# Two Strassen groups of 512 + 512 columns, the last of B's queries among them; heads of both branches in turn with fewer products between; branch A's rotary embedding on GpSimd

## The chip, the cores and the metric

The kernel runs on one core of one Trainium2 chip. The metric is the device time of one execution in microseconds (us); the median of three runs counts.

## The reference, cut to what matters

One encoder block with two token mixers in parallel: branch A is differential attention (8 heads, each with two 64-wide halves), branch B is grouped-query attention (8 query heads over 2 key/value heads) with normed q and k and a two-dimensional rotary embedding. All projections come from one matrix of 2048 x 10752.

```python
h = rmsnorm(x, norm_g)                                   # x: 512 x 2048, float32
qa, ka, va, za, qb, kb, vb, zb, ga, gb = split(h @ w_in) # w_in: 2048 x 10752
qa, ka = apply_rope(qa, ang_1d), apply_rope(ka, ang_1d)
oa = rmsnorm(diff_attention(qa1, qa2, ka1, ka2, va, lam), subln_g) * (1 - lam_init)
ya = (oa * silu(za)) @ w_out_a                           # 1024 x 2048
qb, kb = axial_rope(rmsnorm(qb)), axial_rope(rmsnorm(kb))
yb = (gqa_attention(qb, kb, vb) * silu(zb)) @ w_out_b    # 1024 x 2048
x = x + (sigmoid(ga) * ya + sigmoid(gb) * yb) @ w_o      # 2048 x 2048
return rmsnorm(x, final_g)
```

`apply_rope` is `x * cos` plus the other half of `x` times a signed `sin`: two multiplications and one addition per element.

## The kernel before

Every float32 factor of a large product is split into a high part (`hi`, rounded to the matmul type fp32r, a cast on ScalarE, L103) and a low part (`lo`, what is left, a subtraction on VectorE, L104). One product then takes three matmuls: high by high, low by high, high by low. A weight piece of 512 KB (tile `w_raw`, 128 x 1024) is loaded by an SP queue, cast to `w_hi` and subtracted to `w_lo`; eight `w_raw` buffers (named in the list `slots`) are used in turn.

The program has five stages. First (0 to 69 us of the span) x is loaded, normed and transposed, and four column blocks of 128 are projected. Second, up to 714.5 us, comes the Strassen stage (`strassen`, matmul line L234): each group takes 256 + 256 columns of `w_in` as 2 x 2 quarters and forms 7 products instead of 8. There are four groups of columns (`STRASSEN_BLOCKS`: V of branch A, K and V of B, and B's query blocks 28 to 31), and twelve groups for the gates z and g. A product is 48 matmuls with a moving side of 256 columns for the column groups (x is the stationary side), and 48 as well for the gates, 336 in a group. The `b` quarters are loaded once; differences of quarters (`sub`, L209) are made on VectorE in the place of the loaded ones.

Third is attention (714.5 to 1119 us). The order of TensorE's work is written out by hand here (`manual_schedule`); the other engines' order is set by the scheduler of the language. The sixteen heads come in the order `HEADS`. For each head, TensorE does the scores of four row blocks, the transposes that turn a later head's q (`turn`), the transposes of this head's probabilities (`turn_p`, L608), and later, after the next head's first two score blocks, the product with V (`attend`, L621). Between these pieces stand steps of other work, taken from `fillers()` by `fill(n)`: the three digits of a head in `FILLS` are the steps after `finish` of the head before, before `turn_p`, and after `turn_p`. A step is 12 matmuls of 512 columns or 24 of 256. The middle digit is what TensorE has to do while the last row block of scores is reduced (max), exponentiated and scaled on VectorE and ScalarE, since the fourth transpose of `turn_p` needs that row block.

The steps come from `FILL_BLOCKS`: eight pairs of column blocks of `w_in` with 8 steps each (branch A's q and k blocks as pairs of rows, 96 matmuls of 512 columns; B's query blocks 32, 33 and 34, 35 as pairs of columns, 192 matmuls of 256 columns), and then 32 steps of the output projection `w_out_b`. For `w_out_b`, B's head results (`og`) have to be split into hi and lo first; they fall in the last pair's steps.

`load_roped` prepares q and k of a head of branch A: it loads a block, loads it a second time with its halves exchanged, and does the rotary embedding in place with three `tensor_tensor` of 128 x 512 on VectorE (L546 to L548). It is called twice per head, two heads ahead. Branch B's rotary embedding (`rope_b`) is on VectorE too; the reciprocal root of its norm is two small operations on GpSimd (`rsqrt_pool`, L99 and L100). The last multiplication of an A head (L700) is on GpSimd.

Fourth is `w_out_a` (1119 to 1199 us), fifth the output projection `w_o` in four Strassen groups with the final norm.

The PSUM tiles `acc` and `aux` are eight banks, shared out anew by `share_banks` in each stage.

Of the kernel before, what the change touches and what calls it, by code (L numbers as in the profile page):

```python
# [45 lines left out]
FILLS = "141 141 131 131 030 021 032 142 121 350 121 131 332 331 222 232".split()  # L46
# [3 lines left out]
def hybrid_block_kernel(  # L50
# [8 lines left out]
    nc = tc.nc  # L59
# [4 lines left out]
    ps_pool = ctx.enter_context(tc.tile_pool(name="ps", bufs=1, space=bass.MemoryType.PSUM))  # L64
    banks = {}

    def share_banks(**kw):
        banks.update(kw)

    def bank(kind, shape):  # L70
        ring = banks[kind]
        ring.append(ring.pop(0))
        return ps_pool.tile([P, *shape], F32, name=kind, tag=f"bank{ring[-1]}")

    def acc_tile(*shape):
        return bank("acc", shape)
# [201 lines left out]

    zg = dram.tile([2 * BW, S], F32, name="zg")
# [209 lines left out]

# [45 lines left out]
    def load_roped(b):  # L535
# [550 lines left out]
```

## Time and profile before

| what | us |
|---|---|
| median of 3 runs (1374.53 to 1377.92) | 1374.69 |
| the profiled execution's own time | 1376.67 |
| its span in the trace | 1374.9 |
| Strassen stage | 69.4 to 714.5 |
| attention stage | 714.5 to 1119.0 |
| `w_out_a`, then `w_o` | 1119.0 to 1374.9 |

The span is the time from the first to the last instruction. PE is TensorE, DVE VectorE, ACT ScalarE, POOL GpSimd and SP SyncE, which issues the transfers. In a row of instructions the form is: line, engine, operation, output<-inputs, shape, count. Where a view gives `a, b, c` after a wait, those are the total, the number and the longest.

### The profile page before, as it was taken

Reading aid. Unit: us, or ns where it says so; the run is one execution under the profiler, and the core shown is the slowest. Engines: PE = TensorE matmul, PEld = TensorE weight load, DVE = VectorE, ACT = ScalarE, POOL = GpSimd, SP = SyncE. Lnnn points to the kernel's source line nnn. Section 1 sums busy time; section 2 is a strip of 40 time slices with the busy share of each in tenths; the row PEclk is TensorE's granted clock in tenths of the full one; section 3 lists DMA queues with packets and bytes.
Section 4 is the critical chain, followed back from the end, with each engine's and each line's share of the span. In section 5 each row is a group of like instructions: output and inputs, shape, how many; then the busy total and the mean of one; then the engine's idle time right before and its main releaser. Section 6 shows DMA issues by size and latency. Waiting matters only on the chain.

```text
span 1374.9 us, 24100 instructions
## 1 busy us (share of the span) xinstructions
PE 1350.2 (98%) x9625; PEld 1274.1 (93%) x9625; DVE 1081.1 (79%) x1400; ACT 702.9 (51%) x1110; POOL 84.5 (6%) x94
## 2 busy tenths in 40 slices
PE   6999999999999999999999999999999999999997
PEld 6999999999999999999998888888788888899997
DVE  5977787777777777777759778787898858899886
ACT  7643333444444444444446675575676753354444
POOL 1000000000000000000003201000000010004322
PEclk9999999999999999999999999999999999999999
DMA  8245434543333444333377454545575446463333
GB/s 291 77 147 161 124 116 149 154 146 113 118 121 123 148 149 143 117 122 118 123 207 220 122 154 147 153 139 162 171 221 182 130 145 202 151 245 116 97 95 123
DMA packets 201743, 204.21 MB, mean 149 GB/s; under 512 B 11280, under 2 KB 175392, under 8 KB 200992
## 3 DMA queue, kind: packets, MB, share of 16 engines
q1 hardware_dynamic: 201632, 202.69, 47.5%
q8 instruction: 75, 1.23, 0.4%
q14 instruction: 36, 0.29, 0.1%
HBM read 165.68 MB, written 32.77 MB: 144 GB/s over the span
## 4 chain that ended last, share of the span: by engine, by line
PE 90%; DVE 4%; ACT 2%; DMA 1%; issue 1%; POOL 0%; SPq 0%; DVEq 0%; POOLq 0%; ACTq 0%
PE acc L234 55%; PE acc L175 27%; PE aux L621 3%; PE aux L608 2%; PE aux L739 1%; DVE w_lo L104 1%; PE aux L664 1%; PE aux L665 1%; DVE w_raw L209 1%; DMA rows<-og 1%; DMA xt<-in_x_dram 1%; PE aux L389 0%; DMA rows<-yg 0%; ACT sq L366 0%; ACT w_hi L103 0%
## 5 line engine op out<-in xcount | busy, mean ns | idle before, releaser
L103 ACT CAST w_hi<-w_raw 128x1024 fp32r<-128x1024 f32 x351 | 368.5, 1050 | 516.8 <-PE acc L234 397.9
L104 DVE TENSOR_TENSOR w_lo<-w_raw,w_hi 128x1024 fp32r<-128x1024 f32 x351 | 431.9, 1232 | 168.7 <-ACT w_hi L103 168.2
L209 DVE TENSOR_TENSOR w_raw<-w_raw 128x1024 f32<-128x1024 f32 x160 | 200.0, 1250 | 2.4
L234 PE MATMUL acc<-a2h,w_hi 128*128 128x256 f32 x384 | 108.7, 283 | 0.0
L234 PE MATMUL acc<-a2l,w_hi 128*128 128x256 f32 x384 | 108.7, 283 | 0.0
L234 PE MATMUL acc<-a2h,w_lo 128*128 128x256 f32 x384 | 108.7, 283 | 0.0
L234 PEld LDWEIGHTS acc<-a2h,w_hi 128*128 128x128 f32 x384 | 73.7, 192 | 0.0
L234 PEld LDWEIGHTS acc<-a2l,w_hi 128*128 128x128 f32 x384 | 73.7, 192 | 0.0
L234 PEld LDWEIGHTS acc<-a2h,w_lo 128*128 128x128 f32 x384 | 73.7, 192 | 0.0
L576 DVE TENSOR_REDUCE nmax<-aux 128x1 f32<-128x512 f32 x96 | 61.0, 681 | 7.5 <-PE aux L739 4.7
L175 PE MATMUL acc<-a1h,w_hi 128*128 128x512 f32 (+1 forms) x160 | 56.6, 358 | 0.2 <-ACT a1h L393 0.2
L175 PE MATMUL acc<-a1l,w_hi 128*128 128x512 f32 (+1 forms) x160 | 55.6, 353 | 0.1
L175 PE MATMUL acc<-a1h,w_lo 128*128 128x512 f32 (+1 forms) x160 | 55.7, 353 | 0.0
L175 PE MATMUL acc<-a2l,w_hi 128*128 128x512 f32 (+1 forms) x160 | 55.5, 348 | 0.0
L175 PE MATMUL acc<-a2h,w_hi 128*128 128x512 f32 (+1 forms) x160 | 55.5, 350 | 0.0
L175 PE MATMUL acc<-a2h,w_lo 128*128 128x512 f32 (+1 forms) x160 | 55.4, 347 | 0.0
L234 PE MATMUL acc<-s4h,w_lo 128*128 128x256 f32 x192 | 54.3, 283 | 0.0
L234 PE MATMUL acc<-a1h,w_hi 128*128 128x256 f32 x192 | 54.3, 283 | 0.0
L234 PE MATMUL acc<-a1l,w_hi 128*128 128x256 f32 x192 | 54.3, 283 | 0.0
L234 PE MATMUL acc<-a1h,w_lo 128*128 128x256 f32 x192 | 54.3, 283 | 0.0
L234 PE MATMUL acc<-s1h,w_hi 128*128 128x256 f32 x192 | 54.3, 283 | 0.0
L234 PE MATMUL acc<-s1l,w_hi 128*128 128x256 f32 x192 | 54.3, 283 | 0.0
(325 smaller groups left out, 4356.0 us busy)
## 6 DMA issues: line engine op xcount, KB each, us to landing
w_raw<-in_w_in_dram SPq DMA_DIRECT2D x136, 512.0 KB, 3.6
w_raw<-in_w_in_dram SPq DMA_DIRECT2D x64, 256.0 KB, 3.7
w_raw<-in_w_o_dram SPq DMA_DIRECT2D x32, 512.0 KB, 4.4
gg<-kept SPq DMA_DIRECT2D x32, 256.0 KB, 2.4
w_raw<-in_w_out_b_dram SPq DMA_DIRECT2D x32, 256.0 KB, 3.5
rows<-gg SPq DMA_DIRECT2D x32, 256.0 KB, 3.4
w_raw<-in_w_out_a_dram SPq DMA_DIRECT2D x32, 256.0 KB, 3.4
cols<-pv SPq DMA_DIRECT2D x26, 256.0 KB, 3.3
```

The source lines that it names most:

```text
L103: nc.scalar.copy(out=hi, in_=src)
L104: nc.vector.tensor_tensor(out=lo, in0=src, in1=hi.bitcast(F32), op=ALU.subtract)
L175: nc.tensor.matmul(out=acc[b][:, place], lhsT=l, rhs=r, start=first and kc == order[0] and k == 0 and i == 0, stop=last and kc == order[-1 ...
L209: nc.vector.tensor_tensor(out=d, in0=u, in1=v, op=ALU.subtract)
L234: nc.tensor.matmul(out=ps[u] if by_row else ps[:, u, :], lhsT=l, rhs=r, start=n % (2 if by_row else 4) == 0 and k == 0 and i == 0, stop=n ...
L576: nc.vector.tensor_reduce(out=nmax, in_=sps, axis=AX.X, op=ALU.max, negate=True)
L608: nc.tensor.transpose(out=tp[:, i * P:(i + 1) * P], in_=self.p[i][:, j * P:(j + 1) * P], identity=ident)
L621: nc.tensor.matmul(out=o, lhsT=l, rhs=r, start=j == 0 and i == 0, stop=j == NT - 1 and i == 2)
L664: nc.tensor.matmul(out=sp, lhsT=qs[:, sl], rhs=kh, start=True, stop=False)
L665: nc.tensor.matmul(out=sp, lhsT=qs[:, sl], rhs=kl, start=False, stop=True)
L739: nc.tensor.matmul(out=sp, lhsT=l, rhs=r, start=n == 0, stop=n == 2)
```

## The change

Two of the three column groups after the first, 20 to 27 and 28 to 35 instead of 20 to 23, 24 to 27 and 28 to 31, are formed by a new function `strassen_wide` of 512 + 512 columns. A quarter is 1024 x 512 in four pieces of 512 KB; a product is 48 matmuls of 512 columns with the other factor stationary, and is held in a two-bank PSUM tile. Two of the quarter sets use `w_raw` buffers, a third a pool of its own (`wide`), and the quarter b21 is loaded again for the last product. The first of the two groups (`late`) forms p5 before p2.

B's query blocks 32 to 35 thereby leave `FILL_BLOCKS`, which has six pairs (48 steps) instead of eight (64). `HEADS` has the heads of A and B in closer turn, and `FILLS` has 65 steps after the first 8 instead of 89, so that 7 steps of `w_out_b` are left after the last head (before: none). The rotary embedding of branch A is done by GpSimd. PSUM pools are opened anew for each stage (`new_banks`).

```diff
-STRASSEN_BLOCKS = [(16, 17, 18, 19), (20, 21, 22, 23), (24, 25, 26, 27), (28, 29, 30, 31)]
-FILL_BLOCKS = [(32, 33), (2, 10), (3, 11), (34, 35), (4, 12), (5, 13), (6, 14), (7, 15)]
-HEADS = "B0 B1 A0 B2 B3 B4 B5 A1 A2 B6 B7 A3 A4 A5 A6 A7".split()
+STRASSEN_BLOCKS = [(16, 17, 18, 19)]
+
+WIDE_BLOCKS = [tuple(range(20, 28)), tuple(range(28, 36))]
+FILL_BLOCKS = [(2, 10), (3, 11), (4, 12), (5, 13), (6, 14), (7, 15)]
+HEADS = "B0 B1 A0 B2 B3 A1 B4 B5 A2 B6 A3 B7 A4 A5 A6 A7".split()
...
-FILLS = "141 141 131 131 030 021 032 142 121 350 121 131 332 331 222 232".split()
+FILLS = "121 111 121 111 111 121 111 111 121 111 121 111 222 222 222 222".split()
...
+    def strassen_wide(w, left, right, act, wide, done, late=False):
+        H = NK // 2
+        def load(q, half, pieces):
+            tiles = []
+            for p in range(4):
+                if q < 2:
+                    r = raw_tile(q * 4 + p, (2, S))
+                else:
+                    r = wide.tile([P, 2, S], F32, name="w_raw", tag=f"w_wide{p}")
...
+        def product(name, b):
+            ps = acc_tile(2, S)
+            ah, al = act[name]
+            for p in range(4):
+                hi, lo = split_w(b[p])
+                for u in range(2):
+                    sl = slice(u * P, (u + 1) * P)
+                    for k in range(2):
+                        kk = p * 2 + k
+                        for i, (l, r) in enumerate(((ah, hi), (al, hi), (ah, lo))):
+                            nc.tensor.matmul(out=ps[:, u, :], lhsT=l[:, kk, sl], rhs=r[:, k, :],
+                                             start=kk == 0 and i == 0, stop=kk == H - 1 and i == 2)
+            return ps
...
+        b11, b12 = load(0, 0, left), None
+        if late:
+            b12 = load(1, 0, right)
+        b21 = load(2, 1, left)
+        b12 = b12 or load(1, 0, right)
+        p1 = product("a11", b11)
+        u = tmp("u")
+        nc.scalar.copy(out=u, in_=p1)
+        if not late:
+            p2 = product("a12", b21)
+            b22 = load(2, 1, right)
+        sub(b11, b12, b11)
+        p5 = product("s1", b11)
+        if late:
+            p2 = product("a12", b21)
+            b22 = load(2, 1, right)
+        done(0, 0, plus(tmp("c"), p2, u))
+        sub(b11, b22, b11)
+        p6 = product("s2", b11)
+        plus(u, p6, u)
+        t = plus(tmp("t"), p5, u)
+        sub(b12, b22, b12)
+        p3 = product("s3", b12)
+        b21 = load(1, 1, left)
+        plus(u, p3, u)
+        done(1, 1, plus(tmp("c"), p5, u))
...
+        done(0, 1, plus(t, product("s4", b22), t))
+        sub(b21, b21, b11)
+        done(1, 0, plus(u, product("a22", b21), u))
...
+        with tc.tile_pool(name="wide", bufs=1) as wide:
+            for n, blocks in enumerate(WIDE_BLOCKS):
+                def kept(th, ch, v, blocks=blocks):
+                    keep_cols(blocks[ch * 4:ch * 4 + 4], th * 2, 2, v)
+                strassen_wide(w_in, column_pieces(blocks[:4]), column_pieces(blocks[4:]), xq, wide, kept, late=n == 0)
...
-        nc.vector.tensor_tensor(out=o, in0=o, in1=sa, op=ALU.mult)
-        nc.vector.tensor_tensor(out=v, in0=v, in1=ca, op=ALU.mult)
-        nc.vector.tensor_tensor(out=v, in0=v, in1=o, op=ALU.add)
+        nc.gpsimd.tensor_tensor(out=o, in0=o, in1=sa, op=ALU.mult)
+        nc.gpsimd.tensor_tensor(out=v, in0=v, in1=ca, op=ALU.mult)
+        nc.gpsimd.tensor_tensor(out=v, in0=v, in1=o, op=ALU.add)
```

TensorE's list of instructions has 9152 rows before and 8432 after. In the column groups VectorE's order changes most. Before, a 256 + 256 group reads like this on VectorE (`w_lo` are splits, `w_raw<-w_raw` differences of quarters, `kept<-acc,kept` the sums of products):

```order
L104 TENSOR_TENSOR w_lo<-w_raw,w_hi 128x1024 x2
L209 TENSOR_TENSOR w_raw<-w_raw 128x1024 x2
L104 TENSOR_TENSOR w_lo<-w_raw,w_hi 128x1024
L432 TENSOR_TENSOR kept<-acc,kept 128x512
L209 TENSOR_TENSOR w_raw<-w_raw 128x1024
L104 TENSOR_TENSOR w_lo<-w_raw,w_hi 128x1024
L209 TENSOR_TENSOR w_raw<-w_raw 128x1024
L104 TENSOR_TENSOR w_lo<-w_raw,w_hi 128x1024 x3
L240 TENSOR_TENSOR kept<-acc,kept 128x512 x2
L104 TENSOR_TENSOR w_lo<-w_raw,w_hi 128x1024 x2
L240 TENSOR_TENSOR kept<-acc,kept 128x512
L432 TENSOR_TENSOR kept<-acc,kept 128x512
```

After, the first wide group from the splits of its second product's quarter on (`wide_c` and `wide_u` are the sums, 128 x 1024 now):

```order
L112 TENSOR_TENSOR w_lo<-w_raw,w_hi 128x1024 x6
L310 TENSOR_TENSOR w_raw<-w_raw 128x1024
L112 TENSOR_TENSOR w_lo<-w_raw,w_hi 128x1024
L310 TENSOR_TENSOR w_raw<-w_raw 128x1024 x2
L112 TENSOR_TENSOR w_lo<-w_raw,w_hi 128x1024
L310 TENSOR_TENSOR w_raw<-w_raw 128x1024 x2
L112 TENSOR_TENSOR w_lo<-w_raw,w_hi 128x1024 x2
L310 TENSOR_TENSOR w_raw<-w_raw 128x1024
L330 TENSOR_TENSOR wide_c<-acc,wide_u 128x1024
L112 TENSOR_TENSOR w_lo<-w_raw,w_hi 128x1024
L310 TENSOR_TENSOR w_raw<-w_raw 128x1024
L112 TENSOR_TENSOR w_lo<-w_raw,w_hi 128x1024
```

Differences of quarters now alternate with splits piece by piece, since a quarter has four pieces, and the two L240/L432 sums of 128 x 512 are one L330 sum of 128 x 1024.

The second place is VectorE from the second pair of row blocks of head B5 to the four `pl` that follow its `turn_p` (`nmax` is the row maximum, `rs` one over the sum, `kl` the low part of A's keys, `pl` that of the turned probabilities). Before:

```order
L576 TENSOR_REDUCE nmax<-aux 128x1 x2
L578 TENSOR_TENSOR nmax<-nmax,ssb 128x1
L104 TENSOR_TENSOR kl<-kd,kh 128x512
L578 TENSOR_TENSOR nmax<-nmax,ssb 128x1
L546 TENSOR_TENSOR other<-other,sa 128x512
L744 RECIPROCAL rs<-ssum 128x1 x2
L104 TENSOR_TENSOR w_lo<-w_raw,w_hi 128x1024
L547 TENSOR_TENSOR cols<-cols,ca 128x512
L104 TENSOR_TENSOR pl<-aux,ph 128x512 x4
L548 TENSOR_TENSOR cols<-cols,other 128x512
```

After:

```order
L681 TENSOR_REDUCE nmax<-aux 128x1 x2
L683 TENSOR_TENSOR nmax<-nmax,ssb 128x1
L112 TENSOR_TENSOR kl<-kd,kh 128x512
L683 TENSOR_TENSOR nmax<-nmax,ssb 128x1
L849 RECIPROCAL rs<-ssum 128x1 x2
L112 TENSOR_TENSOR w_lo<-w_raw,w_hi 128x1024
L112 TENSOR_TENSOR pl<-aux,ph 128x512 x4
```

The three rotary operations L546 to L548 are gone from between; the split of `kl` and that of a weight piece stand where they stood.

The third place is GpSimd in the middle of the heads, where `ssb` is the norm of a B head (L99 and L100, now L107 and L108). Before:

```order
L99 TENSOR_SCALAR ssb<-ssb 128x4
L100 TENSOR_TENSOR ssb<-ssb,neg_half 128x4
L700 TENSOR_TENSOR rows<-y_9156,rows 128x512
L99 TENSOR_SCALAR ssb<-ssb 128x4
L100 TENSOR_TENSOR ssb<-ssb,neg_half 128x4
```

After:

```order
L652 TENSOR_TENSOR cols<-cols,ca 128x512
L107 TENSOR_SCALAR ssb<-ssb 128x4
L108 TENSOR_TENSOR ssb<-ssb,neg_half 128x4
L652 TENSOR_TENSOR cols<-cols,ca 128x512
L651 TENSOR_TENSOR other<-other,sa 128x512
L653 TENSOR_TENSOR cols<-cols,other 128x512
```

The rotary operations (now L651 to L653) stand between the two small operations that the B heads' scores need.

## Rows read from the trace of the kernel before

**Rows 1.** The page, busy time of each engine, share of the span, instructions.

```profile
PE 1350.2 (98%) x9625; PEld 1274.1 (93%) x9625; DVE 1081.1 (79%) x1400; ACT 702.9 (51%) x1110; POOL 84.5 (6%) x94
```

**Rows 2.** Stretches: window, length, busy us (count) per engine, PEclk, DMA share, GB/s.

```profile
core 0: us, PE busy (x) PEld busy (x) DVE busy (x) ACT busy (x) POOL busy (x), PEclk, DMA share, GB/s
...
69.40:714.50 645.10, 645.10 (x5378) 645.10 (x5378) 485.72 (x466) 273.16 (x294) 0.00 (x0) 1.00 0.44 136
734.80:920.00 185.20, 184.71 (x999) 159.78 (x998) 146.46 (x282) 121.58 (x268) 14.89 (x15) 0.99 0.53 157
...
1000.00:1119.00 119.00, 118.83 (x563) 98.91 (x562) 105.23 (x180) 84.18 (x164) 6.03 (x4) 1.00 0.56 173
```

**Rows 3.** The chain that ended last, in order: start, us, what.

```profile
714.50 17.29 PE acc L175 x144
...
733.61 1.20 PE aux L587 x8
...
747.97 10.90 PE acc L175 x48
...
1118.96 79.37 PE acc L175 x350
```

**Rows 4.** Waits of TensorE between 714 and 1120 us.

```profile
PE aux L587 <- ACT w_hi L103: 1.8, 1, 1.8
PE acc L175 <- ACT og1h L103: 0.5, 1, 0.5
PE aux L608 <- DVE p L555: 0.5, 1, 0.5
```

**Rows 5.** Groups by form, 690 to 1130 us: busy, mean ns | idle before.

```profile
L548 DVE TENSOR_TENSOR cols<-cols,other 128x512 f32<-128x512 f32 x16 | 12.0, 752 | 0.2
L546 DVE TENSOR_TENSOR other<-other,sa 128x512 f32<-128x512 f32 x16 | 10.9, 680 | 1.8 <-DMA other<-pv 1.8
L547 DVE TENSOR_TENSOR cols<-cols,ca 128x512 f32<-128x512 f32 x16 | 10.9, 684 | 8.4 <-DMA cols<-pv 8.4
...
L700 POOL TENSOR_TENSOR rows<-y,rows 128x512 f32<-128x512 f32 x8 | 13.5, 1686 | 292.8 <-DVE y L699 175.9 <-DMA w_raw<-in_w_out_b_dram 74.3 <-DMA w_raw<-in_w_out_a_dram 29.1
```

**Rows 6.** Groups by form: 400 to 600 us (first row), 1246 to 1263 us (others).

```profile
L209 DVE TENSOR_TENSOR w_raw<-w_raw 128x1024 f32<-128x1024 f32 x40 | 48.8, 1220 | 0.7
...
L209 DVE TENSOR_TENSOR w_raw<-w_raw 128x1024 f32<-128x1024 f32 x6 | 9.4, 1574 | 0.0
L104 DVE TENSOR_TENSOR w_lo<-w_raw,w_hi 128x1024 fp32r<-128x1024 f32 x5 | 8.7, 1759 | 0.0
L944 POOL TENSOR_TENSOR xrh<-xrh,gf 128x256 f32<-128x256 f32 x6 | 8.1, 1369 | 123.0 <-DMA gf<-in_final_g_dram 120.7 <-ACT acc L923 2.3
L944 POOL TENSOR_TENSOR xrl<-xrl,gf 128x256 f32<-128x256 f32 x4 | 6.8, 1721 | 0.0
```

**Rows 7.** GpSimd and VectorE side by side (timeline: start, us, what), and GpSimd alone.

```profile
827.07 2.20 POOL L700 TENSOR_TENSOR rows<-y,rows 128x512 f32<-128x512 f32 x1 [41.38 <-DVE y L699]
...
828.05 1.77 DVE L548 TENSOR_TENSOR cols<-cols,other 128x512 f32<-128x512 f32 x1
...
933.19 1.30 POOL L700 TENSOR_TENSOR rows<-y,rows 128x512 f32<-128x512 f32 x1 [70.19 <-DVE y L699]
```

**Rows 8.** Timeline: last score matmul and last scaling, heads B4, B7 and A6.

```profile
853.50 0.39 PE L739 MATMUL aux<-kbl,qh 128*128 128x512 f32 x1
...
860.10 0.48 DVE L555 TENSOR_SCALAR p<-p,rs 128x512 f32<-128x512 f32 x1
...
970.97 0.40 PE L739 MATMUL aux<-kbl,qh 128*128 128x512 f32 x1
...
974.12 0.49 DVE L555 TENSOR_SCALAR p<-p,rs 128x512 f32<-128x512 f32 x1
...
1074.35 0.39 PE L665 MATMUL aux<-kl,qs 128*128 128x512 f32 x1
...
1080.35 0.74 DVE L673 SCALAR_TENSOR_TENSOR p<-e,rs,p 128x512 f32<-128x512 f32 x1
```

**Rows 9.** Loads of weight pieces: KB each, us to landing; and SyncE's waits, 60 to 700 us.

```profile
w_raw<-in_w_in_dram SPq DMA_DIRECT2D x136, 512.0 KB, 3.6
...
SPq L203 <- DVE w_lo L104: 213.8, 107, 2.8
```

More of the change, by code (lines that the diff above doesn't have):

```diff
@@ L62, in hybrid_block_kernel, with new_banks @@
     dram = ctx.enter_context(tc.tile_pool(name="dram", bufs=1, space=bass.MemoryType.DRAM))
-    ps_pool = ctx.enter_context(tc.tile_pool(name="ps", bufs=1, space=bass.MemoryType.PSUM))
+    ps_pools = ctx.enter_context(ExitStack())
     banks = {}
+    def new_banks(unit):
+        ps_pools.close()
+        banks["pool"] = unit, ps_pools.enter_context(
+            tc.tile_pool(name="ps_" + unit, bufs=1, space=bass.MemoryType.PSUM))
     def share_banks(**kw):
@@ L72, in bank @@
         ring.append(ring.pop(0))
-        return ps_pool.tile([P, *shape], F32, name=kind, tag=f"bank{ring[-1]}")
+        unit, pool = banks["pool"]
+        return pool.tile([P, *shape], F32, name=kind, tag=f"{unit}{ring[-1]}")
     def acc_tile(*shape):
@@ L116, in split_w @@
         if free is None:
-            hi = wp.tile(shape, F32R, name="w_hi", tag="w_hi")
-            lo = wp.tile(shape, F32R, name="w_lo", tag="w_lo")
+            hi, lo = (wp.tile(shape, F32R, name=n, tag=n) for n in ("w_hi", "w_lo"))
         else:
@@ L277, in strassen, with sub, tmp, plus @@
         slots[:] = o[1] + o[0] + o[3] + o[2]
+    def strassen_wide(w, left, right, act, wide, done, late=False):
[7 more added lines that the diff above has]
+                    r = wide.tile([P, 2, S], F32, name="w_raw", tag=f"w_wide{p}")
+                row, at = (half * H + p * 2) * P, 0
+                for c0, n in pieces:
+                    nc.sync.dma_start(out=r[:, :, at:at + n],
+                                      in_=w[row:row + 2 * P, c0:c0 + n].rearrange("(k p) n -> p k n", p=P))
+                    at += n
+                tiles.append(r)
+            return tiles
+        def sub(dst, x0, x1):
+            for d, u, v in zip(dst, x0, x1):
+                nc.vector.tensor_tensor(out=d, in0=u, in1=v, op=ALU.subtract)
+        def product(name, b):
[11 more added lines that the diff above has]
+            return ps
+        def tmp(tag):
+            return wide.tile([P, 2, S], F32, name="wide_" + tag, tag="wide_" + tag)
+        def plus(dst, ps, sb):
+            nc.vector.tensor_tensor(out=dst, in0=ps, in1=sb, op=ALU.add)
+            return dst
+        b11, b12 = load(0, 0, left), None
[24 more added lines that the diff above has]
+        done(1, 1, plus(tmp("c"), p5, u))
+        if late:
+            ring = banks["acc"]
+            ring[0], ring[1] = ring[1], ring[0]
+        done(0, 1, plus(t, product("s4", b22), t))
+        sub(b21, b21, b11)
+        done(1, 0, plus(u, product("a22", b21), u))
@@ L336, in plain_rows @@
         return stream_steps(w_in, column_pieces(blocks), NK, False, act, kept, **kw)
+    new_banks("bank")
     share_banks(acc=[0, 1, 2, 3], aux=[4, 5, 6, 7])
@@ L453, in hybrid_block_kernel @@
             project(STRASSEN_BLOCKS[0], early, in_xt, before={"s2": late_sums})
+        slots[:] = slots[2:4] + slots[0:2] + slots[4:]
+        new_banks("pair")
+        share_banks(acc=[2, 3, 0, 1])
+        with tc.tile_pool(name="wide", bufs=1) as wide:
[3 more added lines that the diff above has]
+                strassen_wide(w_in, column_pieces(blocks[:4]), column_pieces(blocks[4:]), xq, wide, kept, late=n == 0)
+        slots[:] = slots[0:2] + slots[4:6] + slots[2:4] + slots[6:8]
         with tc.tile_pool(name="sp", bufs=6) as sp:
+            new_banks("bank")
+            free = [2 * i + j for i in banks["acc"] for j in range(2)]
+            share_banks(acc=free[:4])
             def tmp():
```

## Prediction

> **What bounds the kernel now.** I read four views in this order. The page's busy times show TensorE at 98% of the span and VectorE at 79% [rows 1], so the sum starts with TensorE's work, and VectorE is what can get in its way. The stretches say where: in the Strassen stage TensorE is busy for all of the 645.10 us, with VectorE at 485.72 (75%); among the heads (734.8 to 920) TensorE has 184.71 of 185.20 and VectorE 79%; from 1000 to 1119 VectorE has 105.23 of 119.00, 88% [rows 2]. TensorE's waits in the attention stage are few: 1.8 us before B0's transposes, one 0.5 for the last scaling of a head's probabilities, one 0.5 for the splits of the head results [rows 4]. [...] The chain gives the pace of a matmul by its width.
>
> **Matmuls removed.** A matmul of 256 columns takes 645.10 / 5378 = 120.0 ns in the Strassen stage [rows 2] and 17.29 / 144 = 120.1 in the first steps of attention; one of 512 columns takes 10.90 / 48 = 227.1, or 79.37 / 350 = 226.8 over the longest piece [rows 3]; I take 226.9. So two narrow ones cost 240, one wide one 227. Of the column groups, three leave: 3 x 336 = 1008 narrow matmuls, 121.0 us. Two pairs of B's queries leave the steps: 2 x 192 = 384 narrow ones, 46.1 us. Two wide groups come: 2 x 7 x 48 = 672 wide ones, 152.5 us. Net **-14.6 us** on the engine that sets the end: 5.8 of the 46.1 is Strassen's eighth product, the rest the fixed part of each matmul. TensorE's list loses just these 720 rows, and no other matmul changes.
>
> **Cover in the heads.** 16 steps (64 - 48) and the order of the heads change what lies between a head's last score matmul and the fourth transpose of its `turn_p`. For seven of the eight B heads (all but B0) the middle digit falls to 1: 12 wide matmuls, 2.73 us, and 0.33 until the fourth transpose. To this come 0.44 where the next head is a B, whose q is turned there (4 transposes at 109 ns), and 0.45 where the head before is an A, whose norm has two matmuls there. So the cover is 3.06 for B1, B3 and B5, 3.5 for B6 and B7, 3.95 for B2 and B4, 3.44 in the mean. Against it stands the latency from the issue end of the last score matmul (its start plus 0.23) to the end of the last scaling. B7 shows the shortest of before, 974.61 - 971.20 = 3.41, and B4 the longest, 860.58 - 853.73 = 6.85 [rows 8]: between B4's two rows VectorE ran almost without a gap through work of others. In the new order nothing but one `kl` (0.68) or one weight split (1.22) stands in the way, partly beside the exponential on ScalarE, and the rotary operations that stood there have gone. Adding these per head by the order's rows gives latencies of 4.15 (B1), 4.6 (B2), 3.55 (B3), 4.15 (B5), 4.0 (B6), and 3.5 or less for B7 and under the cover for B4; less the covers that is 1.1 + 0.65 + 0.5 + 1.1 + 0.5 = 3.85 us. The 0.5 that B4 waits now goes [rows 4]. Net **+3.3**; bounds 0 (all at 3.41: 3 x 0.35, less the 0.5) and 23.9 (all at 6.85: 7 x 3.41). I take the low part since the rows that made B4 slow are those that move to GpSimd.
>
> Six A heads come newly to two middle steps, 5.46 + 0.33 + 0.45 = 6.24 us. A6 has that cover now and takes 1081.09 - 1074.58 = 6.51 [rows 8], a wait of 0.27. Six times that is **+1.6**, bounds 0 and 5. The splits of B's results for `w_out_b` (`og1h`, `og1l`) fall between B7 and A4, in fewer steps than before; they cost one wait of 0.5 [rows 4]. VectorE is the fullest engine in that region [rows 2]; I take three such waits, **+1.5**, bounds 0 and 6.
>
> **Start of the heads.** From the last gate product (714.50) to B0's transposes (733.61) pass 19.1 us for B0's loads, tables and norm [rows 3], and that does not change. The six steps ahead of them shrink from 17.29 to 72 x 0.2271 = 16.35, so TensorE waits **+0.9** longer there, at the most. At the end the seven `w_out_b` steps that the heads now leave over run at the same pace behind them: 0.
>
> **Wide groups.** VectorE has per wide group 28 splits, 16 differences and 6 sums of 128 x 1024, about 50 x 1.22 = 61 us [rows 6] in 336 x 0.2269 = 76.2 of TensorE, 80%; before it was 75% and TensorE waited nowhere [rows 2]. Loads of 512 KB need 3.6 us to land and already wait 107 times for a split to free their buffer [rows 9]. New is that b22 goes into the buffers of b21, issued only when b21 is split, and b21 comes a second time into those of b12, while VectorE, in order, holds a difference that needs them. One product (10.9 us) lies between; a margin of about 1 us is left by the order's rows, so **+1**, bounds 0 and 8 (four fills of a third buffer set, each 2 us late, by the spread of one load).
>
> **Rotary on GpSimd.** VectorE loses 12.0 + 10.9 + 10.9 = 33.8 us and two in-order waits for transfers, 8.4 and 1.8 [rows 5]. GpSimd gets 48 operations of 128 x 512: 1.30 us alone, 2.20 beside VectorE [rows 7], 1.69 in the mean [rows 5], so 62 to 106 us in 400, on an engine that is 6% busy [rows 1]; loads two heads ahead hide them. What they do to VectorE is the open price. Beside GpSimd's multiplications of `xrh` and `xrl` (14.9 us in all), VectorE's subtraction goes from 1220 ns to 1574 and its split to 1759 [rows 6]: eleven operations lose 6 x 0.354 + 5 x 0.54 = 4.8 us, for GpSimd work that alone would be ten times some 0.74, an estimate from half of the 1.30 for half the columns and a fixed part: 7.4 us, so 0.65 us lost per us. A rotary addition took 1.77 beside GpSimd instead of 0.68 [rows 7, 5]. For 62 us that is between 0, if they fall beside VectorE's reading of PSUM and its idle time, and 40. About half of VectorE's time among the heads goes to operations of two operands from SBUF, so I take 20: VectorE still gains 34 + 10 (eight weight splits fewer) - 20. For the single late scaling that falls beside one: **+1**, bounds 0 and, for all of it, the case below.
>
> [...]
>
> **Sum.** -14.6 + 3.3 + 1.6 + 1.5 + 0.9 + 1 + 1 = -5.3 us. The profiled execution's own time is 1376.67 for a span of 1374.9, 2.0 above the median; taken from the median of 1374.7, that is **1369.4 us** (from the profiled execution 1371.4).
>
> **Rivals.**
> (1) The covers hold: latencies near B7's 3.41 and VectorE relieved; 14.6 less 0.9 and some 0 to 3: 1360 to 1364. For it: the rotary rows lie in B4's slow stretch. Against: a cover of 3.06 is under the shortest latency seen.
> (2) VectorE loses the whole 40 us by GpSimd, 20 more than in the sum. Then relief and loss cancel while TensorE has 30 us less in which to hide VectorE's work; of the 20 a third to two thirds falls into the covers: +7 to +13, 1376 to 1382. For it: rows 6. Against: GpSimd's work can fall where VectorE reads PSUM.
> (3) Slower: each of the seven B heads waits in the short cover. The place is the transposes of `turn_p`, the price 7 x (latency - 3.44). The other terms leave 14.6 + 0.5 - 6.0 = 9.1 us to lose, so it decides from a mean latency of 4.75, and the time is over 1378.8 from 5.35. At 5.5, between B7's and B4's: +14.4, 1380. For it: B4's 6.85 with a short cover in the same place. Against: that stretch held the rotary operations.
> (4) The wide groups wait for their late loads at the bound, +8 instead of +1: 1376. Against: no wait on a load in 645 us [rows 2].
>
> **How the numbers follow.** A measurement of this kernel can tell 0.3% from no change: below 1370.6 is faster, above 1378.8 slower. My forecast (1364 to 1373): 0.42, of it 0.32 faster and 0.10 same. (1): 0.20, faster. (2): 0.15, 0.08 same and 0.07 slower. (3): 0.17, 0.05 same and 0.12 slower. (4): 0.06, same. Together 0.52 faster, 0.29 same, 0.19 slower. The range goes from the full gain of (1), 1360, to 1381, past most of (2) and half of (3).
>
> **What would show it.** Matmuls: the column groups take about 152 us in two pieces at 227 ns, without waits. Covers: TensorE's waits L713 <- `p` in the attention stage sum to about 5 us over the B and A heads; 12 or more is (3), under 2 is (1). GpSimd: about 70 to 90 us busy in the heads, and VectorE's `w_lo` among the heads above 1.22 us; at 1.6 or more in the mean it is (2). Wide groups: waits on `w_lo` or on loads of more than 4 us make (4). The forecast is wrong if TensorE's waits in all exceed 13 us more than now, or if the wide matmul's pace in a two-bank tile isn't 227 ns.

## The result

The changed kernel takes 1415.79 us (median of 4) against 1374.99 for the kernel before in the same series: 1.0298 times as long, 95% interval 1.0285 to 1.0311. That is 41 us slower, far outside the predicted range of 1360 to 1381. The profiled execution took 1416.43, its span is 1414.5.

The page of the changed kernel, its engine line and the row of TensorE's clock, beside [rows 1]:

```profile
PE 1350.8 (95%) x8905; PEld 1240.2 (88%) x8905; DVE 1091.4 (77%) x1359; ACT 707.3 (50%) x1111; POOL 152.0 (11%) x142
...
PEclk9999999999999999999999999999789999999999
```

720 matmuls are gone and TensorE is still as long busy (1350.8 for 1350.2), now at 95% instead of 98%: those that are left ran slower in places. The last row is the granted clock in forty slices, in tenths; two of them are at 0.7 and 0.8. The waits of TensorE from 60 us on (engine, what it waited for: total, number, longest), beside [rows 4]:

```profile
PE acc L182 <- ACT og1h L111: 19.0, 5, 10.5
PE aux L713 <- ACT p L658: 7.6, 6, 5.0
PE aux L713 <- DVE p L660: 5.6, 6, 1.5
PE aux L692 <- DMA cols<-pv: 3.6, 1, 3.6
PE aux L713 <- DVE p L778: 1.8, 2, 0.9
PE acc L241 <- DVE wide_u L330: 1.6, 1, 1.6
PE acc L322 <- DVE xt L522: 1.4, 1, 1.4
```

Five waits on `og1h`, the high part of B's head results for `w_out_b`, are the largest item; before, there was one, of 0.5. Fourteen waits before turned probabilities (L713) come next. Three stretches of the changed kernel, beside [rows 2] (the wide groups, the first half of the heads, and the place of the `og1h` waits):

```profile
110.00:264.00 154.00, 152.65 (x675) 126.15 (x673) 119.25 (x103) 60.92 (x58) 0.00 (x0) 1.00 0.53 162
764.00:960.00 196.00, 181.57 (x850) 149.88 (x849) 161.66 (x294) 133.19 (x301) 72.08 (x63) 0.96 0.50 148
1000.00:1035.00 35.00, 16.90 (x57) 11.59 (x56) 14.99 (x28) 12.52 (x26) 7.05 (x5) 0.66 0.44 130
```

The wide groups run almost without a gap. Among the heads TensorE stands 14 us of 196, and in 35 us around 1017 it is busy for 16.9, at a mean granted clock of 0.66 (PEclk is 0.50 from 1008.9 to 1032.8, 1.00 before and behind).

I added up the distances from one matmul's start to the next over the whole span, subtracted the pace of its width at full clock (the prediction's), and sorted what is left by place. Distances at half clock count apart.

| part, us | before | after | change | predicted |
|---|---|---|---|---|
| matmuls at their pace | 1287.3 | 1272.7 | -14.6 | -14.6 |
| waits in the Strassen stage | 0 | 4.5 | +4.5 | +1 |
| wait at the start of the heads | 2.0 | 3.75 | +1.75 | +0.9 |
| transposes of probabilities, B heads | 0.7 | 15.95 | +15.3 | +3.3 and +1 |
| the same, A heads | 0.3 | 2.1 | +1.8 | +1.6 |
| `og1h`, `og1l` before `w_out_b` | 1.3 | 20.6 | +19.2 | +1.5 |
| other waits among the heads | 2.4 | 4.4 | +2.0 | |
| slower matmuls at half clock | 1.5 | 10.8 | +9.3 | none |

The sum is +39.3; the spans differ by 39.6.

**The longest wait.** The chain of the changed kernel (start, us, what) from the last multiplication of head A3 on:

```profile
1006.88 1.28 POOL rows L805
...
1008.17 3.16 DMA og<-rows
...
1011.39 2.87 DMA rows<-og
...
1014.28 0.63 ACT og1h L111
...
1014.93 0.70 DVE og1l L112
...
1015.65 2.67 DMA rows<-og
...
1018.35 0.63 ACT og1h L111
```

A3's result is multiplied in its `z` buffer, stored (3.16 us), and only then does the first reload of an earlier B head's result start, in that buffer: 2.87 us to load, 0.63 and 0.70 to split. The next reload starts when that split has ended, again in the same buffer, since the other `z` buffer is B7's until its last multiplication at 1035 us; four of them stand behind each other at some 4.1 us each. TensorE has reached `w_out_b` and waits for each.

**The wait at B1.** The timeline of the changed kernel around the longest wait before turned probabilities:

```profile
804.64 1.30 POOL L653 TENSOR_TENSOR cols<-cols,other 128x512 f32<-128x512 f32 x1
...
805.97 1.85 DVE L674 TENSOR_TENSOR rope<-cols,ts_q 128x256 f32<-128x256 f32 x2 [3.06 <-POOL cols L653]
...
807.86 1.64 DVE L675 TENSOR_TENSOR cols<-cols,tc_q 128x512 f32<-128x512 f32 x1
809.42 1.27 DVE L681 TENSOR_REDUCE nmax<-aux 128x1 f32<-128x512 f32 x2
...
812.31 1.32 ACT L658 ACTIVATE p<-p,rs 128x512 f32<-128x512 f32 x2
...
813.08 1.30 PE L713 MATMUL aux<-ident,p 128*128 128x128 f32 x3 [5.04 <-ACT p L658]
```

VectorE runs these operations one behind the other, in the order of its list: the rotary of a later B head (L674, from 805.97) stands ahead of B1's last maxima (L681, from 809.42). It waits 3.06 us for GpSimd's rotary addition: what L674 writes and what that addition reads share the two `rope2` buffers. Beside GpSimd's next operations the two L674 then take 1.85 us together and L675 1.64 (in `rot_v` 0.86 for two and 0.68, in the mean). Only after that do the maxima and the scaling follow. By heads, the idle time before the transposes is 5.2 us at B1, 2.4 at B4, 2.6 at B6 and 3.2 at the other five B heads together.

### The profile page after: what moved, and what is told of

It is laid out like the page before. It is cut to its first block, busy times and chain, and to the rows that moved or that the text cites. A ratio compares the mean times of both kernels' runs of the same rounds, so it can differ in the third digit from the quotient of the medians.

```text
span 1414.5 us, 22730 instructions
## 1 busy us (share of the span) xinstructions
PE 1350.8 (95%) x8905; PEld 1240.2 (88%) x8905; DVE 1091.4 (77%) x1359; ACT 707.3 (50%) x1111; POOL 152.0 (11%) x142
## 4 chain that ended last, share of the span: by engine, by line
PE 78%; DVE 8%; ACT 5%; DMA 4%; issue 3%; POOL 1%; SPq 1%; POOLq 0%; DVEq 0%; ACTq 0%
PE acc L241 44%; PE acc L182 18%; PE acc L322 10%; PE aux L726 2%; PE aux L713 1%; DVE w_lo L112 1%; DMA rows<-og 1%; ACT p L684 1%; PE aux L769 1%; PE aux L770 1%; DMA cols<-pv 1%; DVE nmax L681 1%; ACT w_hi L111 1%; DVE w_raw L216 1%; DMA xt<-in_x_dram 1%
## 5 line engine op out<-in xcount | busy, mean ns | idle before, releaser
L111 ACT CAST w_hi<-w_raw 128x1024 fp32r<-128x1024 f32 x357 | 375.3, 1051 | 523.1 <-PE acc L241 317.2
L112 DVE TENSOR_TENSOR w_lo<-w_raw,w_hi 128x1024 fp32r<-128x1024 f32 x357 | 442.3, 1241 | 176.0 <-ACT w_hi L111 175.5
L216 DVE TENSOR_TENSOR w_raw<-w_raw 128x1024 f32<-128x1024 f32 x136 | 170.7, 1255 | 2.0
L681 DVE TENSOR_REDUCE nmax<-aux 128x1 f32<-128x512 f32 x96 | 61.1, 682 | 14.8 <-PE aux L770 8.3
L182 PE MATMUL acc<-og1h,w_hi 128*128 128x512 f32 x128 | 51.9, 406 | 19.0 <-ACT og1h L111 19.0
L241 PE MATMUL acc<-s1h,w_lo 128*128 128x256 f32 x192 | 54.5, 284 | 0.9 <-DVE nlam L579 0.9
L241 PE MATMUL acc<-s2h,w_lo 128*128 128x256 f32 x192 | 54.4, 283 | 0.0
L241 PE MATMUL acc<-s3h,w_hi 128*128 128x256 f32 x192 | 54.4, 283 | 0.0
```

Source lines behind the costliest of these rows:

```text
L111: nc.scalar.copy(out=hi, in_=src)
L112: nc.vector.tensor_tensor(out=lo, in0=src, in1=hi.bitcast(F32), op=ALU.subtract)
L182: nc.tensor.matmul(out=acc[b][:, place], lhsT=l, rhs=r, start=first and kc == order[0] and k == 0 and i == 0, stop=last and kc == order[-1 ...
L216: nc.vector.tensor_tensor(out=d, in0=u, in1=v, op=ALU.subtract)
L241: nc.tensor.matmul(out=ps[u] if by_row else ps[:, u, :], lhsT=l, rhs=r, start=n % (2 if by_row else 4) == 0 and k == 0 and i == 0, stop=n ...
L681: nc.vector.tensor_reduce(out=nmax, in_=sps, axis=AX.X, op=ALU.max, negate=True)
```

## The experiments

Where no ratio stands, the time is that of a single execution; the others are medians, with a ratio to the kernel before, timed beside them. Executions of one kernel lie up to 6 us apart (`kq_rot_v_mid2`: 1373.88 to 1380.25), so a smaller difference to a single time is not shown by the times; there the waits in the traces have to carry the argument. Names of waits: `og1h` are the reloads, "transposes" the waits on `p`.

### Three causes taken apart: rotary, order of heads, buffers

`rot_v` undoes one part of the change. It sets theory G against theory Z, which is about the reloads. Theory G: the waits before turned probabilities, 18 us in the changed kernel, come from the rotary's operations on GpSimd, for whose tiles VectorE waits, as the 3.06 us at B1; they fall to 6 us or less, and the time to 1395 or less.

```diff
-        nc.gpsimd.tensor_tensor(out=o, in0=o, in1=sa, op=ALU.mult)
+        nc.vector.tensor_tensor(out=o, in0=o, in1=sa, op=ALU.mult)
```

(and so the other two operations). 

> The changed kernel with the rotary of branch A back on VectorE, nothing else. [...] Theory Z (the reload of head results for w_out_b waits for the two z buffers, one of which a head of branch A holds): the 20.6 us of waits on og1h stay at 18 or more, and the time stays above 1400.

Measured: 1402.38, 13.4 less. TensorE's waits:

```profile
PE acc L182 <- ACT og1h L111: 18.7, 5, 10.2
...
PE aux L713 <- ACT p L658: 3.5, 6, 2.0
PE aux L713 <- DVE p L660: 3.1, 4, 1.3
```

The waits on `p` fall from 15 to 8.4 us, the `og1h` waits stay. Theory Z holds for the reloads, theory G for part of the other waits.

`b7_first` exchanges two heads.

```diff
-HEADS = "B0 B1 A0 B2 B3 A1 B4 B5 A2 B6 A3 B7 A4 A5 A6 A7".split()
+HEADS = "B0 B1 A0 B2 B3 A1 B4 B5 A2 B6 B7 A3 A4 A5 A6 A7".split()
```

> The changed kernel with only the heads A3 and B7 exchanged, so that B7 follows B6 directly, as before the change; rotary still on GpSimd. Theory Z: the waits on og1h fall from 20.6 us to under 6, and with them most of the 24 us stretch at half clock; time about 1390. Theory G: waits on og1h stay at 15 or more, time within 5 us of 1416.

Measured: 1407.1. The `og1h` waits fall from 19.0 to 6.4, so A3 between B6 and B7 was most of it. But 9 us came back in place of the 26 expected: the slower matmuls at half clock, sorted as in the table, fell by less than 1 us, and other waits grew, those of A heads' transposes (L778) from 1.8 to 4.5:

```profile
PE acc L182 <- ACT og1h L111: 6.4, 3, 3.4
...
PE aux L713 <- DVE p L778: 4.5, 4, 1.6
```

`og_kq` changes one buffer name.

```diff
-                hi_lo(*og_act(k), load_rows(og, k, "z", 2))
+                hi_lo(*og_act(k), load_rows(og, k, "kq", 2))
```

> The changed kernel with the reloads of head results taken into the kq buffers instead of the z buffers. Theory Z: reloads start as soon as the og tiles are free; waits on og1h fall from 20.6 us to under 6, time about 1390. Theory G, or if the loads themselves are the limit: 15 us or more stay.

Measured: 1394.98, 20.8 less. No wait on `og1h` is left, one of 1.2 on `og1l`. So it was the `z` buffer, not the load's own duration and not GpSimd, whose rotary is unchanged here. The waits on `p` stay, at 16.6.

`before_rot_g` makes the converse edit on the kernel before: only L546 to L548 on GpSimd. 

> The kernel before with only the rotary of branch A moved to GpSimd. Theory G: slower by 8 us or more, with waits before turned probabilities of 8 us or more. Rival (it costs only together with short covers): within 4 us of 1375, waits under 4 us, since the covers there are two to four steps.

Measured: 1388.78, ratio 1.0096 (1.0079 to 1.0113), 12 to 13 us slower. The price is that of `rot_v`, with other heads and covers. But it does not show where theory G put it: before turned probabilities there is one wait of 1.7, and the largest new one is that of an A head's norm:

```profile
PE aux L689 <- ACT sqh L103: 4.6, 1, 4.6
...
PE aux L608 <- DVE p L555: 1.7, 1, 1.7
```

Its timeline tells where that wait comes from:

```profile
816.26 1.28 ACT L649 ACTIVATE qs<-cols 64x512 fp32r<-64x512 f32 x2 [7.35 <-POOL cols L548]
816.92 1.10 DVE L650 SCALAR_TENSOR_TENSOR qs<-cols,qs 64x512 fp32r<-64x512 f32 x1 [5.49 <-ACT qs L649]
```

ScalarE, in order, waits 7.35 us for GpSimd's rotary addition of a later A head's q, VectorE 5.49 us behind it, and the norm's `sqh` comes only after that, at 822.70. In the kernel before, `sqh` stands ahead of that `qs` (816.21):

```profile
815.69 0.63 ACT L103 CAST sqh<-osq 128x512 fp32r<-128x512 f32 x1
```

### Do the causes add up, and what is left

`kq_rot_v` has both edits, `og_kq` and `rot_v`. 

> Both at once: reloads in the kq buffers and rotary back on VectorE, the rest as changed. If the two causes are independent, the savings seen apart, 13 and 21 us, add up: 1416 - 34 = 1382, with TensorE's waits before turned probabilities at about 8 us and none on og1h. If they shared a cause (one stall counted twice), 1388 or more.

Measured: 1380.98; apart they saved 13.4 and 20.8, together 34.8. They add up, so no stall was counted twice.

`kq_rot_v_mid2` then moves one step of each of the seven B heads ahead of the transposes.

```diff
-FILLS = "121 111 121 111 111 121 111 111 121 111 121 111 222 222 222 222".split()
+FILLS = "121 120 121 120 120 121 120 120 121 120 121 120 222 222 222 222".split()
```

> The kernel of kq_rot_v with the last step of the seven B heads moved from behind the transposes to ahead of them (111 becomes 120): cover 5.8 instead of 3.1 us. Theory C (the short cover is what the remaining waits before turned probabilities are): they fall from 8 to 3 us or less, time 1376. Rival (VectorE is late anyway, so that the wait only moves to the scores or to attend): the time stays within 2 us of kq_rot_v.

Measured: 1376.2, ratio to before 1.0001 (0.9989 to 1.0012). The waits of B heads' transposes fall as theory C has it: those on ScalarE's `p` from 3.5 to 0.7, those on L660 (4.5) are gone. New ones of 2.8 appear where the next scores now stand directly behind the transposes. In time it is 4.8 us less than the single execution of `kq_rot_v`, but 1.2 between the two profiled executions, so how much of the waits came back as time is not shown.

`kq_rot_g_mid2` is the same with the rotary on GpSimd. 

> The kernel of kq_rot_v_mid2 with the rotary on GpSimd, as the change has it. Theory G: 8 to 13 us slower than kq_rot_v_mid2, as in the two pairs seen, so it does not depend on the covers. If GpSimd's price were only that of short covers: within 4 us.

Measured: 1391.53, 15.3 more than that median, 11.8 more than its profiled execution. A cover twice as long does not take GpSimd's price away.

### Where the saved matmuls go

`heads_b` keeps only the wide groups and B's queries in them: rotary on VectorE, `HEADS` as before the change, and

```diff
+FILLS = "131 121 121 121 030 021 022 122 121 130 121 222 232 222 232 222".split()
```

> Only the wide groups and the four queries in them: rotary on VectorE, the heads in their order of before, and of before's fills 17 steps taken out where covers are longest (131 121 121 121 030 021 022 122 121 130 121 222 232 222 232 222). Theory: the matmuls saved arrive, -14.6, less 4.8 for waits of the wide groups and some 4 us in the heads: 1369, faster than before. If the saved steps themselves were the cover of VectorE: 1376 or more.

Measured: 1383.08, ratio 1.0055 (1.0038 to 1.0072): the removed steps were cover in before's order of heads too. 7.0 us are waits on `og1h`. `heads_b_kq` takes them out. 

> heads_b (only the wide groups; rotary on VectorE; before's order of heads) with reloads in the kq buffers. Theory: the 7 us of waits on og1h go, and some 4 us of half clock: 1383 - 9 = 1374. If the wait lies in the reload itself and not in the z buffers: 1381 or more.

Measured: 1380.13. The `og1h` waits are gone, but only some 3 us came back instead of 9 (`heads_b` lay between 1381.28 and 1386.13). The timeline of `heads_b_kq` at B7 (and the wait of TensorE that follows) shows why:

```profile
971.29 0.69 DVE L112 TENSOR_TENSOR og0l<-rows,og0h 128x512 fp32r<-128x512 f32 x1 [2.83 <-ACT og0h L111]
971.90 0.15 DVE L683 TENSOR_TENSOR nmax<-nmax,ssb 128x1 f32<-128x1 f32 x1
...
981.45 0.48 PE L713 MATMUL aux<-ident,p 128*128 128x128 f32 x1 [5.00 <-DVE p L660]
```

The splits of reloads (`og0l`) stand in VectorE's queue between B7's maxima and scalings, and VectorE waits 2.83 us in order for ScalarE's cast of a reload, which itself waited for the load; TensorE, which no longer waits for the split, waits for B7's probabilities.

`first7` is `kq_rot_v_mid2` with one step more for B0's preparation; B0's last step is dropped for it (`121` becomes `120`).

```diff
-FILL_FIRST = 6
+FILL_FIRST = 7
```

> kq_rot_v_mid2 with seven steps instead of six ahead of B0's transposes (taken from the steps left over behind the heads; B0's last step is dropped, so that all later ones stay in their place). Theory: the 2.5 us wait on B0's loads goes, and with it the stretch at half clock behind it (some 2 us): 1376.2 - 4.5 = 1372. Rival (B0's preparation itself is held up by more work ahead of it): 1376.

Measured: 1379.72, inside the spread of `kq_rot_v_mid2`, so no gain is shown. The wait on B0's loads (2.4) did go, and less time passed at half clock (mean granted clock 0.996 for 0.994 in the profiled executions), but the step that was dropped behind B0 cost 4 us in waits at B0's transposes and product.

`one_pool` is `first7` with a wide product in two one-bank tiles, so that no PSUM pool is closed and opened around the wide groups.

```diff
-            ps = acc_tile(2, S)
+            ps = [acc_tile(S) for _ in range(2)]
...
-        new_banks("pair")
-        share_banks(acc=[2, 3, 0, 1])
+        share_banks(acc=[4, 5, 6, 7, 0, 1, 2, 3])
```

> first7 with a wide product held in two one-bank PSUM tiles, so that the PSUM pool isn't closed and opened around the wide groups. Theory: the waits at the two borders of the wide stage (1.5 and 1.8 us on xt and wide_u) come from the pool's closing and go: 3 us less than first7. Rival (the banks are simply still in use): no change.

Measured: 1376.38, 3.3 less than `first7`, both single times; in the traces the waits on `xt` and `wide_u` (1.4 and 1.6) are gone. That fits the closing and opening of PSUM pools; the smaller tiles came in the same edit and are not told apart from it.

`best` and `best2` move single steps in `one_pool` (`best`: `121` at B7 and `232` at A4; `best2`: `121` at B0, `120` at A1, `232` at A4). 

> one_pool with a step behind the transposes of B7 and one more ahead of those of A4 (from the steps left over), where TensorE still waits 2.1 and 2.8 us. Expected 4 us below one_pool: 1365, about 0.7% under the kernel before.

 

> one_pool with its steps placed otherwise: B0's last step back, A1's last step dropped instead, and three steps ahead of A4's transposes. The waits at B0's attend (2.0), B1's pieces (2.0) and A4's transposes (2.8) should go: 1376 - 5 = 1371, a little faster than before. If the waits only move on, as in best: 1374 or more.

Measured: 1375.02, ratio 0.9993 (0.9982 to 1.0003), and 1374.74, ratio 0.9988 (0.9979 to 0.9998). Each wait that was aimed at went, and others of 2 to 3 us took its place (`og1h` 3.0 in `best`; 2.3 on `w_out_b`'s result and 2.8 at A4's scores in `best2`).

`wide1` asks whether a wide group pays when no step leaves the heads: the kernel before with one wide group for columns 20 to 27, in one PSUM pool. 

> The kernel before with one wide group (columns 20 to 27) in place of two narrow ones, in one PSUM pool; heads, steps, B's queries and the rotary as before the change. 672 matmuls of 256 columns (80.6 us) become 336 of 512 (76.2). Theory H (the lost gain is lost in the heads, where the removed steps were cover): -4.4 + 1.4 for a wait at the third product = -3, 1372. Rival W (wide groups don't pay): 1375 or more.

Measured: 1374.51, ratio 0.9989 (0.9978 to 0.9999), 1.9 us less (0.1 to 3.0 by the interval) where 3 was expected. The Strassen stage has no wait at all and takes 640.7 us instead of 645.1, the 4.4 of the sum. Behind it there is one new wait of 2.0, in the steps before B0; the one of 1.8 at B0's transposes [rows 4] is down to 0.2:

```profile
PE acc L182 <- DVE w_lo L112: 2.0, 1, 2.0
```

So a wide group pays in its own stage what the sum says, and theory H stands; in the whole time the gain is barely clear of noise.

`other_kq` is the changed kernel with the exchanged copy in the `kq` buffers instead of `rope2`. 

> The changed kernel with the exchanged copy of the rotary in the kq buffers instead of sharing rope2 with branch B's rotary; rotary on GpSimd. If GpSimd's price is the shared buffer (VectorE's queue stands for it, as before B1's maxima): the 5.2 us wait before B1's turned probabilities goes and the waits there fall from 15 to 10 us, time 1410. If it is VectorE's slower operations: they stay within 3 us, and the time too.

Measured: 1420.32. VectorE's wait on GpSimd before B1 is gone, but B1's transposes still wait 5.4 us: the same place in VectorE's queue now waits for a load of `cols`. The shared buffer alone is not GpSimd's price.

### A kernel faster than both

`best3` moves another step (`120` at A2, `121` at B7). 

> best2 with A2's last step moved behind B7's transposes. If the waits are local, the 2.99 us wait at A4's scores goes and little comes: 1372, 0.3% below the kernel before. If the steps are cover in all places alike, another wait takes its place: 1374 to 1375.

 Measured: 1373.21, ratio 0.9983 (0.9974 to 0.9992). The wait at A4's scores went, that on `w_out_b`'s result grew from 2.3 to 3.6.

`hb2` has two wide groups in one pool, reloads in `kq`, rotary on VectorE, and before's order of heads.

```diff
-HEADS = "B0 B1 A0 B2 B3 A1 B4 B5 A2 B6 A3 B7 A4 A5 A6 A7".split()
-FILL_FIRST = 6
-FILLS = "121 111 121 111 111 121 111 111 121 111 121 111 222 222 222 222".split()
+HEADS = "B0 B1 A0 B2 B3 B4 B5 A1 A2 B6 B7 A3 A4 A5 A6 A7".split()
+FILL_FIRST = 7
+FILLS = "121 121 121 121 030 021 022 121 121 130 131 222 222 222 222 121".split()
```

> heads_b_kq in one PSUM pool, seven steps ahead of B0, and steps given to B7 (131), where it waited 6.7 us: fills 121 121 121 121 030 021 022 121 121 130 131 222 222 222 222 121. If the waits are local: 1380 - 2.4 - 3.3 - 6 = 1368. If the removed steps are cover in all places alike: 1373 or more.

Measured: 1367.16, ratio 0.9935 (0.9917 to 0.9952), 0.65% faster than the kernel before. Its page and its largest waits from the heads on:

```profile
PE 1338.4 (98%) x8905; PEld 1233.2 (90%) x8905; DVE 1096.2 (80%) x1421; ACT 706.1 (52%) x1113; POOL 83.9 (6%) x94
```

```profile
PE aux L712 <- DVE p L777: 3.0, 5, 1.2
...
PE aux L712 <- ACT p L657: 1.7, 2, 1.4
```

The same 8905 matmuls as in the changed kernel now take 1338.4 us of busy time instead of 1350.8, for the most part since the clock stays up (PEclk 1.00 in the mean from 735 to 1155 instead of 0.95; 1.5 us of slower matmuls instead of 10.8), and 11.8 less than before. By the same addition as above, some 7.5 us of the 14.6 are still given back in small waits in the profiled execution, the slowest of four; by the medians it is 5.5. From `best3`, timed beside it, `hb2` differs in `HEADS` and `FILLS` alone: the 6 us between the two are the places of the heads and steps.

## Why the prediction was wrong

**Right.** The matmuls saved: -14.6 by the pace of the changed kernel too, one wide group after the other:

```profile
111.62 146.92 PE acc L322 x647
```

that is 227.1 ns each. The duration of GpSimd's work (62 to 106 us; the three groups of rows below add up to 71.2).

**Right in the number, by luck: the A heads' covers.** +1.6 was forecast as six waits of 0.27, 1.8 was measured, but as two waits of 0.9, at A4 and A6; A6 is not one of the six heads whose cover is new, and the other five of these do not wait.

**Failed: the term "+1.5" for B's results.** The prediction counted the splits (`og1h`, `og1l`) as VectorE work and priced them by the one wait of before. It did not follow where their inputs come from: the reload needs a `z` buffer, there are two, and the new order of heads lets A3 hold one until its last multiplication on GpSimd, with the store behind it. The upper bound of 6 was set without that chain. +19.2 was measured; `og_kq` shows the buffer as the cause, `b7_first` the order.

**Failed: the term "+3.3" for the covers.** The covers were counted rightly (3.06 to 3.95), the latencies too low: they were put together from B7's undisturbed 3.41 and single operations. +15.3 was measured; the waits are 5.2 us at B1 (forecast 1.1), 2.4 at B4 (0) and 2.6 at B6 (0.5). `rot_v` shows 6.6 us of it to be the rotary on GpSimd, `kq_rot_v_mid2` that most of the rest goes from this place with a longer cover. The rotary's rows left VectorE's queue, but what was behind them was not the only thing late: the prediction looked for the instructions between two rows and not for what these wait for (a load, GpSimd, a reload). This is rival (3), which had 0.17; its price of 14.4 at a latency of 5.5 is near what came, but the total went past it by the two other items.

**Missing: the clock.** The prediction let waits cost their length alone. In the long waits of the changed kernel and for some us behind them the granted level is 0.5 (from 811.0 to 817.8 at the wait of 5.0 us before B1, which ends at 813.1; PEclk 0.66 from 1000 to 1035), and there a matmul of 512 columns takes 0.43 us, against 2.73 / 12 = 0.227 elsewhere in the chain of the same kernel:

```profile
821.84 2.73 PE aux L726 x12
...
1028.71 0.43 PE aux L769
```

10.8 us in all (1.5 before), a fifth on top of the table's 51.3 us of waits. No row of the range spoke for that; the one stretch among the heads of before that shows it is a wait of 2.0 us at their start, with 3.4 us at half clock behind it (PEclk 0.50 from 734.8 to 738.2), and the prediction gave it no price.

**Mis-sized: the wide groups, +1.** 4.5 was measured, not by loads as the prediction feared: two of the three waits stand where PSUM pools are closed and opened around the groups, and go in `one_pool`.

**Mis-sized: the start of the heads, +0.9 "at the most".** 1.75 was measured. The wait on B0's loads, 3.6 here, is 1.8 to 3.1 in nine other runs with the same six steps ahead of it, so part of the excess is scatter.

**Failed: the term "+1" for GpSimd.** The 20 us of VectorE time that the prediction took for the two engines getting in each other's way, its estimate from rows 6 and 7, were about right; the step from there to the time was not. They were set off against the 44 us that VectorE gains, with one late scaling left over. The groups by form among the heads, changed kernel:

```profile
L112 DVE TENSOR_TENSOR w_lo<-w_raw,w_hi 128x1024 fp32r<-128x1024 f32 x45 | 58.9, 1311 | 21.0 <-ACT w_hi L111 20.9
L112 DVE TENSOR_TENSOR pl<-aux,ph 128x512 fp32r<-128x512 f32 x64 | 41.0, 681 | 0.4 <-ACT ph L111 0.4
...
L660 DVE TENSOR_SCALAR p<-p,rs 128x512 f32<-128x512 f32 x16 | 11.3, 713 | 0.5
L674 DVE TENSOR_TENSOR rope<-cols,ts_q 128x256 f32<-128x256 f32 x16 | 9.9, 637 | 3.1 <-POOL cols L653 3.1
...
L683 DVE TENSOR_TENSOR nmax<-nmax,ssb 128x1 f32<-128x1 f32 x32 | 8.6, 271 | 0.0
```

and GpSimd's three:

```profile
L652 POOL TENSOR_TENSOR cols<-cols,ca 128x512 f32<-128x512 f32 x16 | 24.2, 1519 | 115.1 <-DMA cols<-pv 71.4 <-DVE pl L112 40.0 <-DVE w_lo L112 3.7
L651 POOL TENSOR_TENSOR other<-other,sa 128x512 f32<-128x512 f32 x16 | 23.8, 1489 | 27.4 <-DMA other<-pv 27.1
L653 POOL TENSOR_TENSOR cols<-cols,other 128x512 f32<-128x512 f32 x16 | 23.2, 1452 | 1.3
```

and `rot_v`, its page and the same VectorE operations:

```profile
PE 1344.5 (96%) x8905; PEld 1236.2 (88%) x8905; DVE 1098.3 (78%) x1407; ACT 706.6 (50%) x1111; POOL 79.3 (6%) x94
```

```profile
L112 DVE TENSOR_TENSOR w_lo<-w_raw,w_hi 128x1024 fp32r<-128x1024 f32 x48 | 59.4, 1238 | 27.2 <-ACT w_hi L111 27.1
L112 DVE TENSOR_TENSOR pl<-aux,ph 128x512 fp32r<-128x512 f32 x64 | 40.7, 680 | 0.0
...
L660 DVE TENSOR_SCALAR p<-p,rs 128x512 f32<-128x512 f32 x16 | 7.6, 482 | 0.2
...
L674 DVE TENSOR_TENSOR rope<-cols,ts_q 128x256 f32<-128x256 f32 x16 | 6.4, 430 | 0.1
...
L683 DVE TENSOR_TENSOR nmax<-nmax,ssb 128x1 f32<-128x1 f32 x32 | 4.7, 148 | 0.0
```

The page of `rot_v` has VectorE busy for 1098.3 us, 32.5 of it the rotary (10.9, 10.9 and 10.7 in its groups by form); without that 1065.8, against 1091.4 in the changed kernel, 25.6 more. Added up by form over all operations that both kernels have, it is some 21. Of these, `w_lo` loses 45 x 0.073 = 3.3 and `rope` 16 x 0.207 = 3.3; but L683, the step from a B head's maximum to its exponential, loses 32 x 0.123 = 3.9, and L660, its last scaling, 16 x 0.231 = 3.7. These two stand in the chain that TensorE's transposes wait for. The prediction's sign for such a loss, `w_lo` at 1.6 us, looked at an operation that is not in that chain.

So 21 to 26 us of VectorE's time cost 13.4 us: about half, within the third to two thirds that rival (2) took for its share; the forecast counted one late scaling. On TensorE's side, 6.6 of the 13.4 are waits on `p`, and some 4 are slower matmuls at half clock (PEclk 0.95 from 735 to 1155, 0.97 in `rot_v`). The move costs 12 to 15 us in three pairs of kernels. "Loads two heads ahead hide them" did not hold either: ScalarE and VectorE, in order, waited for GpSimd's rotary, 3.1 us in the changed kernel (at B1), 13.1 in two waits in `before_rot_g`, never where the rotary is on VectorE. The shared `rope2` buffer alone isn't the price (`other_kq`). How it divides between slower operations and waits in order was not measured.

The chance also leaned the wrong way because the price of each wait was worked out alone. `best`, `best2` and `best3` show that they are coupled: a step moved to one wait was missed at another. The 16 steps that left the heads were not only part of the work saved but 16 pieces of cover; `hb2`, with the reloads, the rotary and the pools put right as well, gets 9 of the 14.6 us, 6 of them over `best3` by placing heads and steps as it does.

## What to carry to other kernels

Before a step that hides a latency is removed, follow the hidden chain back to its buffers and loads, not only to the instructions between two rows: a buffer that another head holds can put a store, a load and a split in a row, as the 4.1 us per reload here. Where TensorE's work shrinks and another engine's does not, the saved time is gained only if the pieces that are left are placed again. Price a wait with what the clock does after it, from the stretches of the same trace in which it fell. And when work on one engine slows another, count the loss at the operations that somebody waits for; set off against the busy time that was freed, it seems to vanish.

## What the runs showed of the hardware

The changed kernel and `rot_v` differ in the engine of the rotary alone; GpSimd is busy for 152.0 us in the one and 79.3 in the other. Among the heads three VectorE operations with both inputs in SBUF took longer in the changed kernel, in the mean of their groups (`w_lo` 1311 ns for 1238, `rope` 637 for 430, L683 271 for 148), and so did the scaling L660 (713 for 482); `pl`, which takes an input from PSUM, did not (681 for 680). In size the 72.7 us more of GpSimd's busy time cost VectorE 21 to 26 us, about 0.3 us per us, where the tail of the kernel before, in which VectorE did little else than such operations, had let the prediction estimate 0.65 [rows 6].

In the changed kernel TensorE's granted clock was at half (PEclk 0.50) for 24 us around the five waits on `og1h` (1008.9 to 1032.8), for 6.8 us at the wait of 3.6 us before B0 (770.0 to 776.8), for 6.8 us at that of 5.0 before B1 (811.0 to 817.8), and for 3.4 us behind two waits of 1.0 and 1.4 us close together at B4 (909.9 to 913.4). In `hb2`, whose longest wait among the heads is 1.4 us, PEclk is 1.00 in the mean from 735 to 1155, and the mean granted clock of the profiled execution is 0.997; the kernel before, with its 3.4 us at half among the heads, has 0.997 as well, the changed kernel 0.983.
